# A transformer layer with expert retrieval: gathered rows of v from the end of u's loop on, and their sums emptied five chunks ahead of the end

## The chip, the cores and the metric

The kernel runs on one core of one Trainium2 chip. The metric is the device time of one execution in microseconds (us). TensorE (PE) multiplies matrices, VectorE (DVE) and ScalarE (ACT) do elementwise work, GpSimd (POOL) does some of that and issues the gathers, and SyncE (SP) issues most of the large loads.

## The reference

One layer over 256 tokens of width 1024: a mixer (retention beside block attention, merged by gates), and behind it the part that matters here, a product-key retrieval of experts (PEER). Each token picks 128 of 16384 experts (8 heads, 16 each); an expert is one row of u and one row of v:

```python
def one_chunk(args):
    hc, ec, gc = args                                  # tokens, chosen experts, gates
    u = u_tab[ec]
    a = jax.nn.gelu(jnp.einsum('td,thkd->thk', hc, u), approximate=False)
    return jnp.einsum('thk,thkd->td', gc * a, v_tab[ec])
```

The tables u and v are 16384 x 1024 float32 each.

## The kernel before

The tokens are shared between two ways of doing this.

**Dense.** For most tokens (NA = 128 columns in the product with u, ND = 176 in that with v) the kernel goes through the whole tables, in NK = 128 chunks of 128 experts. *u's loop* multiplies each chunk of u with the tokens (L1271) after its transposition on TensorE (L738, copied out by ACT in L739); ACT takes the gelu and POOL multiplies with the gates into W (L1228, L1229). Its last iterations also prepare v's first chunks. *v's loop* multiplies each chunk of v with W and adds up in PSUM. Since the product goes through two halves of reduced precision, each chunk of v is cut on ACT (the high half `rhi`, L148) and DVE (the low half `rlo`, L149), two chunks ahead of its use (`cut_v(c + 2)`), and W likewise once for two chunks (`cut_w`, L1243 and L1244). A chunk is eight pairs of matmuls (L1303, L1304). Six pairs of chunks (PLAIN) go uncut (L1301). The cut halves have four buffers each, the loaded chunks of both tables six (`raw_ring`). The two last chunks of v are done together, block by block, behind the loop, and each block goes through `add_up` (ACT L1349, DVE L1350) and `turn_back` (a transposition, DVE's adds, the writing of the result).

**Gathered.** For NG = 64 tokens all 128 rows of u and of v (as 64 gathers, two rows' worth of tokens in the 128 partitions), and for some more tokens extra gathers, are fetched by index from HBM: NU = 128 gathers of u, 128 rows of 4 KB each, and NV = 80 of v. A fetched tile of u is multiplied with the token and summed on DVE (`dot_v`, L1040). When all dots are done, their gelu and the gates give the weights `av` (L1100, L1101). A fetched tile of v is added to a running sum with its weight (L1115 on DVE; the first one of each sum is a copy on ACT, L1112). There are two running sums: `accx` (the first 16 tiles of v) and `vacc` (the other 64).

The fetched tiles lie in a ring of RING = 6. The gathers go by steps: `gather_step` does one fetch and one dot, or one fetch and one sum, as they come. A fetch is issued on POOL's queue and waits there until DVE is done with the tile that lay in its slot six fetches before; a sum waits on DVE until its tile has landed. Each engine works strictly in the order in which the program lists its instructions, so a step's place in the program sets what waits behind it. How many steps there are is set by a credit: `gather(n)` adds n and does a step for every whole unit. In u's loop n is 1.04 for each chunk, from the point where the top-16 of all tokens is done 1.2 (after a pause of four steps). In v's loop it is 0.65.

A dot of u begins when five tiles of u are outstanding, or when all of u are fetched; so the last four steps of u's part do a dot each and fetch nothing. The last six chunks of u's loop do no steps at all. In v's loop a step fetches until all 80 are fetched, and it sums when six tiles are outstanding or when all are fetched. In chunk NK - 8 = 120 all sums that are left are done at once. Behind them POOL loads the residual: `r0` (64 tokens, L1327), `r0b` (L1331), `r1` (128 tokens, L1332) and `upper`, the upper half of `vacc` (L1333). In chunk 123 `accx` is added to the PSUM sums by 16 matmuls (L1337). In chunk 124 DVE adds `vacc` to `r0` (L1340), in chunk 125 `upper` (L1342), and SP writes the 64 tokens out.

The code of the last chunks:

Of the kernel before, what the change touches and what calls it, by code (L numbers as in the profile page):

```python
# [28 lines left out]
NK = 128  # L29
# [8 lines left out]
RING = 6  # L38
# [25 lines left out]
NU = NJ + NX  # L64
# [12 lines left out]
def layer_kernel(ctx, tc, x, mix_norm_g, w_in, ret_w_branch, moba_q_gain, moba_k_gain, moba_w_branch,  # L77
# [640 lines left out]
    def load_to(i):  # L718
        while state["loaded"] < i + AHEAD + 2 * (i + AHEAD > sk_at):
            load_any(state["loaded"])  # L720
            state["loaded"] += 1

    def transpose_u(c):

        if c < NK and early_chunk(c):
            u_T[c] = u_raw.pop(c)
        elif c in TURN:
            r = u_raw.pop(c)
            u_T[c] = hi_tile(F32)
            for k in range(0, KC, 4):  # L730
                turn(u_T[c], r, slice(k, k + 4))
        elif c < NK:
            r = u_raw.pop(c)
            u_T[c] = hi_tile(F32)
            for q in range(2):
                p = side()
                for k in range(4):
                    T.transpose(p[:, k * P:(k + 1) * P], r.rearrange("p (i k) -> p k i", k=KC)[:, 4 * q + k], ident)  # L738
                A.activation(u_T[c][:, 512 * q:512 * (q + 1)], p, AF.Copy)  # L739
# [55 lines left out]
    for t in range(NT):  # L795
        for q in range(2):
            c = slice(512 * q, 512 * (q + 1))
# [109 lines left out]
    gs = {"n": 0, "u": 0, "dot": 0, "v": 0, "sum": 0, "rows": {}, "x": 0, "soft": False, "xdone": False, "later": [], "pause": 0, "pace": GATHER}  # L907
# [3 lines left out]
    v_order = [*range(NJ, NV), *range(NJ)]  # L911
# [104 lines left out]
    def chain_step(us):  # L1016

        credit["chain"] = min(credit["chain"], 0.0) + us
        while chain and credit["chain"] > 0:
            try:  # L1020
                credit["chain"] -= next(chain[0])
            except StopIteration:
                chain.pop(0)

    def fetch(tab, j):
        n = gs["n"] % RING
        gs["n"] += 1
        r = tk.tile([P, D], F32, name="rows_", bufs=2) if n >= 4 else hp_.tile([P, D], F32, name="rows", tag=("hl", "hh")[n % 2], bufs=2)
        G.indirect_dma_start(out=r, out_offset=None, in_=tab,  # L1029
                             in_offset=bass.IndirectOffsetOnAxis(ap=eg[:, j:j + 1], axis=0))  # L1030
        gs["rows"][j] = r
# [11 lines left out]
    def weights_x():  # L1043

        c = slice(NJ, NU)
        A.activation(av[:, c], av[:, c], AF.Gelu)
        gs["x"] = 0

        def product():
            V.tensor_tensor(av[:, c], av[:, c], gg[:, c], op=OP.mult)  # L1050
            nc.gpsimd.dma_start(gx[1].rearrange("n h i k -> (h i) n k"), av[:, c].rearrange("p (n k) -> p n k", n=NXG))
            after(2, back)

        def back():
            for n in range(NXV, NXG):
                nc.gpsimd.dma_start(x_rows(gates, n), gx[1][n].rearrange("h i k -> i h k"))
            gs["xdone"] = True

        after(2, product)
# [13 lines left out]
    def after(n, f):  # L1073
        gs["later"].append((n, f))

    def later():
        now, gs["later"] = gs["later"], []
        for n, f in now:
            f() if n <= 1 else after(n - 1, f)

    def gather_step():
        later()
        if gs["pause"] > 0:
            gs["pause"] -= 1
            return
        if gs["x"] == NX and gs["soft"]:
            weights_x()
        if gs["dot"] < NU:
            if gs["u"] < len(ready):
                fetch(peer_u[0], ready[gs["u"]])  # L1090
                gs["u"] += 1
            if gs["dot"] < gs["u"] and (gs["u"] - gs["dot"] == RING - 1 or gs["u"] == NU):
                j = ready[gs["dot"]]
                r = gs["rows"].pop(j)
                h = h2 if j < NJ else h2r[(j - NJ) // TOPK]
                after(1, partial(dot_v, j, r, h))
                gs["dot"] += 1
                if gs["dot"] == NU:
                    later()
                    A.activation(av[:, :NJ], av[:, :NJ], AF.Gelu)  # L1100
                    V.tensor_tensor(av[:, :NJ], av[:, :NJ], gg[:, :NJ], op=OP.mult)  # L1101
            return
        if gs["v"] < NV:
            fetch(peer_v[0], v_order[gs["v"]])
            gs["v"] += 1
        if gs["sum"] < gs["v"] and (gs["v"] - gs["sum"] == RING or gs["v"] == NV):
            j = v_order[gs["sum"]]
            r = gs["rows"].pop(j)
            if j in (0, NJ):
                a = cp.tile([P, D], F32, name="vacc", tag="h2") if j == 0 else tk.tile([P, D], F32, name="accx", tag="hx")  # L1110
                gs["acc" if j == 0 else "accx"] = a
                A.activation(a, r, AF.Copy, scale=av[:, j:j + 1])  # L1112
            else:
                a = gs["acc" if j < NJ else "accx"]
                V.scalar_tensor_tensor(a, r, av[:, j:j + 1], a, op0=OP.mult, op1=OP.add)  # L1115
            gs["sum"] += 1
# [46 lines left out]
    def gates_finish():  # L1163
        while full:
            gates_evac(*full.pop())
# [83 lines left out]
    def rows_x(n):  # L1249

        if n < NXG:
            h2r.append(lo_tile(F32))
            nc.scalar.dma_start(h2r[n], h2y[n].rearrange("h i d -> (h i) d"))

    for c in range(NK):
        load_to(len(pieces) + c + TAHEAD)
        rows_x(c)
        gates_finish()
        transpose_u(c + TAHEAD)
        if c and c % 2 == 0:  # L1260
            product_evac(c - 2, pa)
        if c == SCRATCH:
            while any(g in chain for g in topk_all):
                chain_step(1.0)
        if c % 2 == 0:
            pa = acc(0)
        uT = u_T.pop(c)
        hT = hTd if c in TURN or early_chunk(c) else hTf
        for k in range(KC):
            n = c % 2 * NA  # L1270
            T.matmul(pa[:, n:n + NA], uT[:, k * P:(k + 1) * P], hT[:, k], start=(c % 2 == 0 and k == 0),  # L1271
                     stop=(k == KC - 1), skip_group_check=True)
        pump()
        if c < NK - 6:
            gather(gs["pace"])
        chain_step(BUDGET)

        if c == NK - 4:
            while chain:
                chain_step(9.0)  # L1280
                gates_finish()
            cw = cp.tile([P, 2, D], F32R, name="cw", tag="b8")[:, :, :4 * ND].rearrange("p s (c t) -> p s c t", c=2)
        if c >= NK - 5:
            load_to(len(pieces) + c + 3)
        if c == NK - 3:
            cut_w(0)
            cut_v(0)
        elif c == NK - 2:
            cut_v(1)
# [17 lines left out]
    for c in range(NK):  # L1307
        load_to(len(pieces) + NK + c + 2)
        if (c + 2) // 2 not in PLAIN:
            cut_v(c + 2)  # L1310
            if c % 2 == 0:
                cut_w(c + 2)
        if c // 2 in PLAIN:
            cuts[c] = (v_raw.pop(c), None, W[:, c, :])
        else:
            cuts[c] = (*v_cut.pop(c), w_cut[c - c % 2][:, c % 2])
        if c < NK - 2:
            for b in range(KC):
                block(b, c)
            del cuts[c]  # L1320
        gather(GATHER_V)
        if c == NK - 8:
            while gs["sum"] < NV:
                gather_step()

            r0 = tk.tile([P, D], F32, name="rows_", bufs=2)
            nc.gpsimd.dma_start(r0[:NG], x1d[:NG, 0, :])  # L1327
            upper = hp_.tile([P, D], F32, name="rows", tag="hh", bufs=2)
            r1 = hp_.tile([P, D], F32, name="rows", tag="hh", bufs=2)
            r0b = oh_more.rearrange("p a b i j -> p (a b i j)").bitcast(F32)  # L1330
            nc.gpsimd.dma_start(r0b[:half], x1d[NG:, 0, :])  # L1331
            nc.gpsimd.dma_start(r1, x1d[:, 1, :])  # L1332
            nc.gpsimd.dma_start(upper[:NG], gs["acc"][NG:])  # L1333
        if c == NK - 5:

            for b in range(KC):
                T.matmul(o[b][:, 2 * ND:2 * ND + NXP], gs["accx"][:, b * P:(b + 1) * P], pick, start=False, stop=True,  # L1337
                         skip_group_check=True)
        if c == NK - 4:
            V.tensor_tensor(r0[:NG], r0[:NG], gs["acc"][:NG], op=OP.add)  # L1340
        if c == NK - 3:
            V.tensor_tensor(r0[:NG], r0[:NG], upper[:NG], op=OP.add)  # L1342
            nc.sync.dma_start(out_flat[:NG, :], r0[:NG])

# [81 lines left out]
```

## Time and profile before

| | |
|---|---|
| median of 3 runs | 962.13 us (961.7 to 962.34) |
| the profiled execution | 962.2 us |
| its span, first to last instruction | 960.4 us |
| TensorE busy | 942.4 us (98%) |
| VectorE busy | 794.3 us (83%) |
| ScalarE busy | 519.2 us (54%) |
| GpSimd busy | 393.9 us (41%) |
| HBM | 307.52 MB read, 334 GB/s over the span |
| mean granted clock of TensorE | 0.991 |

The times in the profile's rows count from the first instruction. u's loop ends and v's begins near 656 us. A row of a timeline is the start, the duration, the engine, the line, the operation, what is written from what, their sizes and the number of instructions in the row; in brackets stands how long the engine had been idle before it and what ended that. A row of the chain of waits is a start, a duration and what the time went to.

### The profile page before, as it was taken

To read this page: it belongs to the slowest core of one execution; us is meant where nothing else is said; L and a number is where in the kernel's file an instruction comes from. 1 tells how busy PE (TensorE), PEld (TensorE's weight loads), DVE (VectorE), ACT (ScalarE), POOL (GpSimd) and SP (SyncE) were. 2 spreads that over 40 slices of the span, in tenths; PEclk is the share of its full clock that TensorE was granted. 3 is DMA by queue.
4 is the path that set the end of the run, shared out by engine and by line. 5 is a ranking of instruction groups with operands and counts; after the bars stand their busy time and mean duration, and the time that the engine had idled before them with its cause. 6 is when DMAs were issued, how large, how long until landed. Compare 5 with 4: busy or idle time off the path is not lost.

```text
span 960.4 us, 19130 instructions
## 1 busy us (share of the span) xinstructions
PE 942.4 (98%) x7208; PEld 902.6 (94%) x7208; DVE 794.3 (83%) x1514; ACT 519.2 (54%) x956; POOL 393.9 (41%) x303
## 2 busy tenths in 40 slices
PE   8999999999999999999999999999999999999968
PEld 6887898998999999999999998999999999999967
DVE  6567567878679996999799999966798988989885
ACT  5554745544654345444577776966455454545431
POOL 3422010000204455344355675744375656566540
PEclk9999999999999999999999999999999999999987
DMA  9878879998898999999999999998999999999991
GB/s 318 234 191 246 231 223 279 308 308 247 250 396 330 408 360 341 397 359 393 367 369 378 405 367 360 344 361 277 377 409 386 408 378 409 386 393 397 379 332 45
DMA packets 109418, 320.40 MB, mean 334 GB/s; under 512 B 11372, under 2 KB 22517, under 8 KB 109198
## 3 DMA queue, kind: packets, MB, share of 16 engines
q1 hardware_dynamic: 64492, 184.43, 53.5%
q0 software_dynamic: 32512, 115.54, 32.3%
q10 hardware_dynamic: 12322, 19.21, 6.8%
q8 instruction: 57, 0.93, 0.4%
q14 instruction: 35, 0.29, 0.1%
HBM read 307.52 MB, written 13.14 MB: 334 GB/s over the span
## 4 chain that ended last, share of the span: by engine, by line
PE 57%; POOL 18%; issue 14%; DVE 6%; DMA 3%; ACT 1%; POOLq 0%; SPq 0%; DVEq 0%
PE acc L1271 17%; POOL rows L1029 11%; PE side L738 7%; PE acc L231 6%; PE acc L232 6%; PE acc L233 6%; PE acc L240 3%; PE acc L241 3%; PE acc L242 3%; DVE rows L1040 2%; DVE oh_more L1152 1%; DMA rows__5904<-in_peer_u_dram,eg 1%; DMA rows<-in_peer_v_dram,eg 1%; PE side L635 1%; DMA rows__6318<-in_peer_u_dram,eg 1%
## 5 line engine op out<-in xcount | busy, mean ns | idle before, releaser
L1029 POOL DMA_INDIRECT rows<-in_peer_v_dram,eg x54 | 106.9, 1980 | 73.9 <-DVE vacc L1115 48.3
L1029 POOL DMA_INDIRECT rows<-in_peer_u_dram,eg x86 | 103.7, 1205 | 80.6 <-DVE rows L1040 38.0
L738 PE MATMUL side<-ident,raw_ring 128*128 128x128 f32 x800 | 107.4, 277 | 0.4 <-ACT rhi__6591 L739 0.4
L738 PEld LDWEIGHTS side<-ident,raw_ring 128*128 128x128 f32 x800 | 96.9, 192 | 0.5 <-ACT rhi__6591 L739 0.5
L1243 ACT ACTIVATE cw<-W 128x352 fp32r<-128x352 f32 x58 | 28.9, 498 | 67.9 <-PE acc L1304 67.9
L1157 ACT ACTIVATE oh_buf<-oh_more,tS 128x128 bf16<-128x128 f16 x176 | 58.9, 428 | 0.2 <-DVE oh_more L1152 0.2
L1115 DVE SCALAR_TENSOR_TENSOR vacc<-rows,av,vacc 128x1024 f32<-128x1024 f32 x43 | 55.0, 1280 | 3.1 <-DMA rows<-in_peer_v_dram,eg 3.0
L1040 DVE SCALAR_TENSOR_TENSOR rows<-rows,h 128x1024 f32<-128x1024 f32 x43 | 52.7, 1236 | 3.3 <-DMA rows<-in_peer_u_dram,eg 3.3
L1229 POOL TENSOR_TENSOR W<-W,gl 128x256 f32<-128x256 f32 (+18 forms) x29 | 24.4, 842 | 55.6 <-ACT gl L1228 43.2
L1244 DVE TENSOR_TENSOR cw<-W,cw 128x352 fp32r<-128x352 f32 x58 | 30.2, 522 | 17.2 <-ACT cw L1243 16.4
L581 POOL DMA_DIRECT2D x1d<-xt x1 | 0.7, 657 | 88.5 <-DVE xt L563 88.5
L1214 ACT ACTIVATE W<-acc 128x512 f32<-128x512 f32 (+19 forms) x44 | 17.0, 387 | 34.6 <-DVE W L1212 28.9
L1152 DVE TENSOR_TENSOR oh_more<-iota,tI 128x1024 f16<-128x1024 f16 x44 | 33.8, 768 | 0.0
L1153 DVE TENSOR_TENSOR oh_buf<-oh_more,tM 128x1024 f16<-128x1024 f16 x44 | 31.7, 720 | 2.2
L155 POOL TENSOR_TENSOR gny<-va,minus_half 128x8 f32<-128x8 f32 x2 | 4.3, 2126 | 66.7 <-DVE va L455 66.7
L1271 PE MATMUL acc<-hTd,raw_ring 128*128 128x128 f32 x256 | 31.2, 275 | 0.0
L1271 PEld LDWEIGHTS acc<-hTd,raw_ring 128*128 128x128 f32 x256 | 29.9, 192 | 0.0
L1198 PE MATMUL acc<-oh_buf 128*128 128x128 bf16 x176 | 25.7, 219 | 1.5 <-ACT oh_buf L1157 0.7
L1199 PE MATMUL acc<-oh_buf 128*128 128x128 bf16 x176 | 25.7, 219 | 0.0
L1199 PEld LDWEIGHTS <-oh_buf 128*128 128x128 f16 x176 | 19.7, 114 | 3.3 <-issue 1.6
L1231 ACT ACTIVATE W<-acc 128x256 f32<-128x256 f32 (+18 forms) x53 | 19.2, 361 | 5.5 <-PE acc L1271 4.4
L1198 PEld LDWEIGHTS <-oh_buf 128*128 128x128 f16 x176 | 19.8, 114 | 0.0
(2701 smaller groups left out, 3494.0 us busy)
## 6 DMA issues: line engine op xcount, KB each, us to landing
raw_ring<-in_peer_v_dram SPq DMA_DIRECT2D x128, 512.0 KB
raw_ring<-in_peer_u_dram SPq DMA_DIRECT2D x100, 512.0 KB
raw_ring<-in_w_in_dram SPq DMA_DIRECT2D x52, 512.0 KB
raw_ring<-in_peer_w_q_dram SPq DMA_DIRECT2D x16, 512.0 KB
raw_ring<-turned SPq DMA_DIRECT2D x16, 512.0 KB
W<-in_peer_u_dram SPq DMA_DIRECT2D x12, 512.0 KB
eraw<-in_peer_u_dram ACTq DMA_DIRECT2D x32, 128.0 KB
h<-in_peer_u_dram ACTq DMA_DIRECT2D x32, 128.0 KB
```

Of the source, the lines that this page charges most:

```text
L231: T.matmul(o[t], xh[:, s], wh, start=(k == 0), stop=False)
L232: T.matmul(o[t], xh[:, s], wl, start=False, stop=False)
L233: T.matmul(o[t], xl[:, s], wh, start=False, stop=(k == kc - 1))
L738: T.transpose(p[:, k * P:(k + 1) * P], r.rearrange("p (i k) -> p k i", k=KC)[:, 4 * q + k], ident)
L1029: G.indirect_dma_start(out=r, out_offset=None, in_=tab, in_offset=bass.IndirectOffsetOnAxis(ap=eg[:, j:j + 1], axis=0))
L1040: V.scalar_tensor_tensor(r, r, 1.0, h, op0=OP.mult, op1=OP.mult, accum_out=av[:, j:j + 1])
L1115: V.scalar_tensor_tensor(a, r, av[:, j:j + 1], a, op0=OP.mult, op1=OP.add)
L1152: V.tensor_tensor(hot, iota4[:, None].to_broadcast(shape), tI[:, t, :, None, k:k + 4].to_broadcast(shape), op=OP.is_equal)
L1157: A.activation(o1[:, j], hot[:, 0, :, j], AF.Copy, scale=tS[:, t, k + j:k + j + 1])
L1198: T.matmul(p[:, j * P:(j + 1) * P], hi, o1, start=True, stop=False)
L1199: T.matmul(p[:, j * P:(j + 1) * P], lo, o1, start=False, stop=True)
L1271: T.matmul(pa[:, n:n + NA], uT[:, k * P:(k + 1) * P], hT[:, k], start=(c % 2 == 0 and k == 0), stop=(k == KC - 1), skip_group_check=True)
```

## The change

It has three parts. In a step at which all tiles of u are fetched but not all dots done, a tile of v is fetched, if the undone dots and the fetched tiles of v together leave a slot of the ring. In the last six chunks of u's loop the steps go on, if all dots are done and fewer than five tiles of v are outstanding. And the emptying of the sums moves from chunk 120 to chunk 123, with the loads of the residual behind it; the two adds to `r0` move from chunks 124 and 125 to 126 and 127. The 16 matmuls with `accx` stay in chunk 123.

```diff
@@ gather_step
             if gs["u"] < len(ready):
                 fetch(peer_u[0], ready[gs["u"]])
                 gs["u"] += 1
+            elif gs["u"] == NU and NU - gs["dot"] + gs["v"] < RING:
+                fetch(peer_v[0], v_order[gs["v"]])
+                gs["v"] += 1
             if gs["dot"] < gs["u"] and (gs["u"] - gs["dot"] == RING - 1 or gs["u"] == NU):
@@ u's loop
         pump()
-        if c < NK - 6:
+        if c < NK - 6 or gs["dot"] == NU and gs["v"] - gs["sum"] < RING - 1:
             gather(gs["pace"])
@@ v's loop
         gather(GATHER_V)
-        if c == NK - 8:
+        if c == NK - 5:
             while gs["sum"] < NV:
                 gather_step()
...
             nc.gpsimd.dma_start(upper[:NG], gs["acc"][NG:])
-        if c == NK - 5:
-
             for b in range(KC):
                 T.matmul(o[b][:, 2 * ND:2 * ND + NXP], gs["accx"][:, b * P:(b + 1) * P], pick, start=False, stop=True,
                          skip_group_check=True)
-        if c == NK - 4:
+        if c == NK - 2:
             V.tensor_tensor(r0[:NG], r0[:NG], gs["acc"][:NG], op=OP.add)
-        if c == NK - 3:
+        if c == NK - 1:
             V.tensor_tensor(r0[:NG], r0[:NG], upper[:NG], op=OP.add)
             nc.sync.dma_start(out_flat[:NG, :], r0[:NG])
```

## The prediction

> **What bounds the kernel now.** I read the page's shares first, then a table of stretches, then the timelines of TensorE (PE), VectorE (DVE), GpSimd (POOL) and ScalarE (ACT) at the two places that the change touches.
>
> ```profile
> span 960.4 us, 19130 instructions
> PE 942.4 (98%) x7208; PEld 902.6 (94%) x7208; DVE 794.3 (83%) x1514; ACT 519.2 (54%) x956; POOL 393.9 (41%) x303
> ```
> ```profile
> 640.00:657.00 17.00, 17.00 (x153) 17.00 (x153) 6.44 (x10) 9.06 (x20) 2.96 (x3) 1.00 0.71 228
> 700.00:720.00 20.00, 20.00 (x149) 20.00 (x148) 19.82 (x21) 11.51 (x14) 14.77 (x6) 1.00 1.03 409
> 929.80:935.20 5.40, 0.04 (x1) 0.04 (x1) 3.58 (x4) 0.00 (x0) 0.52 (x1) 0.50 0.77 149
> 935.20:946.90 11.70, 11.70 (x49) 11.70 (x50) 7.67 (x8) 1.44 (x2) 0.00 (x0) 0.50 0.21 46
> ```
>
> The columns are the stretch, its length, the busy time of PE, weight load, DVE, ACT and POOL, the granted clock, the DMA share and GB/s. TensorE is full nearly everywhere. In v's loop, DVE (19.82 of 20) and DMA (1.03) are full beside it. At the end of u's loop DMA has room (0.71). The one large hole in PE is 929.8 to 935.2, followed by 11.7 us at half clock. Both lie where the gathered sums are emptied:
>
> ```profile
> 922.59 0.36 PE L1303 MATMUL side<-cw,rhi__10164 128*128 128x352 f32 x1
> 924.77 0.35 PE L1303 MATMUL side<-cw,rhi__10188 128*128 128x352 f32 x1
> 926.95 0.36 PE L1303 MATMUL side<-cw,rhi__10229 128*128 128x352 f32 x1
> 935.16 0.52 PE L1304 MATMUL side<-cw,rlo__10230 128*128 128x176 f32 x1 [7.86 <-DVE rlo__10230 L149]
> 939.02 1.79 PE L1337 MATMUL side<-pick,accx 128*128 128x16 f32 x8
> 942.36 0.64 PE L1303 MATMUL side<-cw,rhi__10250 128*128 128x352 f32 x1
> 946.49 0.55 PE L1303 MATMUL side<-cw,rhi__10272 128*128 128x352 f32 x1
> 948.87 0.35 PE L1303 MATMUL side<-cw,rhi__10300 128*128 128x352 f32 x1
> ```
> ```profile
> 920.36 1.22 DVE L149 TENSOR_TENSOR rlo__10189<-raw_ring,rhi__10188 128x1024 fp32r<-128x1024 f32 x1
> 921.93 1.28 DVE L1115 SCALAR_TENSOR_TENSOR vacc<-rows,av,vacc 128x1024 f32<-128x1024 f32 x1
> ...
> 932.69 1.28 DVE L1115 SCALAR_TENSOR_TENSOR vacc<-rows,av,vacc 128x1024 f32<-128x1024 f32 x1 [1.82 <-DMA rows<-in_peer_v_dram,eg]
> 933.89 1.22 DVE L149 TENSOR_TENSOR rlo__10230<-raw_ring,rhi__10229 128x1024 fp32r<-128x1024 f32 x1
> 940.28 1.21 DVE L1340 TENSOR_TENSOR rows__10221<-rows__10221,vacc 64x1024 f32<-64x1024 f32 x1
> 942.55 1.21 DVE L1342 TENSOR_TENSOR rows__10221<-rows__10221,rows 64x1024 f32<-64x1024 f32 x1
> ```
>
> Seven sums stand in a row on DVE from 921.93 (first and last shown), the last of them waiting for a gathered row. Chunk 123's low half (rlo__10230) stands behind them, so PE, which began that chunk at 926.95, stops for 7.86 us. The clock then falls, and chunk 124 takes 942.36 to 946.49, 4.13 us, where chunk 121 took 922.59 to 924.77, 2.18 us. The two last chunks, which are done together, begin at 948.87.
>
> **The change, part by part.** *How far the rows get ahead.* In u's loop the pace 1.04 is paid for 62 chunks (the code switches in chunk 61) and 1.2 for 60: 64.48 + 72.0 = 136.48, so 136 steps by chunk 121 (128 fetches, 4 pauses, 4 steps that drain the dots) and a credit of 0.48. Each of the 4 draining steps now fetches a row of v too (undone dots plus v rows are 4, under the ring's 6). Chunk 122 adds 1.2, one step: the fifth row. Then 5 rows are outstanding and the new condition (under 5) stops it. V's loop starts with 5 rows fetched, none summed, credit 0.68. Before, after s steps s rows were fetched and s − 5 summed; now s + 5 are fetched and s summed. Before, chunk 120 had 0.48 + 0.65 × 121 = 79.1, so 79 steps and 74 sums, its own and six emptied: the seven seen. Now the 80th sum needs 0.68 + 0.65 × (c + 1) ≥ 80, chunk 122, and the last fetch (step 75) is in chunk 114. The emptying, moved to chunk 123, finds nothing left. That holds for any credit, as 0.65 × 124 = 80.6.
>
> *What goes.* Sums 75 to 80 spread over chunks 115 to 122 at the old pace, so chunk 123's low half follows in its turn. From 926.95, at full clock: chunk 123, 2.18; the 16 matmuls of L1337, 942.36 − 939.02 = 3.34 at half clock, so 1.67; chunks 124 and 125, 4.36. Together 8.21, so the last two begin at 935.16 and not at 948.87: 13.7 us saved. The 11.5 us behind them stay.
>
> *The rule on the clock.* The Trainium skill, page "TensorE: Matmul & The Clock Gate", Part 1, says that the clock is gated after about 3.4 us of idleness and comes back after about 3.4 us of sustained work. The trace has 11.7 us of full work at 0.50 behind the stop, more than three times that; by the page the slow part would have cost 3.4 / 2 = 1.7 us, and the gain would be 7.9 + 1.7 = 9.6 us. The measured stretch decides the sum.
>
> *What the five fetches cost in u's loop.* On POOL, ahead of what is queued there:
>
> ```profile
> 633.22 1.25 POOL L1029 DMA_INDIRECT rows<-in_peer_u_dram,eg  x1 [0.16 <-issue]
> 638.28 0.73 POOL L1229 TENSOR_TENSOR W<-W,gl 128x256 f32<-128x256 f32 x1 [3.81 <-ACT gl L1228]
> 646.88 0.74 POOL L1229 TENSOR_TENSOR W<-W,gl 128x256 f32<-128x256 f32 x1 [7.88 <-ACT gl L1228]
> ```
> ```profile
> 645.31 0.26 ACT L1100 ACTIVATE av<-av 128x64 f32<-128x64 f32 x1 [4.14 <-DVE rows L1040]
> 645.47 1.07 ACT L739 ACTIVATE rhi__7333<-side 128x512 f32<-128x512 f32 x2
> 648.28 1.95 PE L1271 MATMUL acc<-hTf,rhi__7333 128*128 128x128 f32 x16
> ```
>
> A fetch there is 1.25 us. The fetches of rows 0 and 1 stand between the last u row (633.22) and the product at 638.28, rows 2 and 3 ahead of that at 646.88, where POOL idles 3.81 and 7.88 us: covered. A fetch first waits until the dot of the row six before is done (its ring slot); those are dots of rows 122 to 126, one or more steps old. Without that cover each would delay the products, and through them the release of PSUM, by at most its 1.25 us. The five rows are 2.6 MB, 6.4 us at 409 GB/s, in 17 us with a DMA share of 0.71, so 4.9 us of room in it. The loads on SP's queue get slower by that, but each is issued six chunks of 2.7 us ahead. The place to watch is ACT at 645.31: it stands 4.14 us for the last dot, which waits for its row; the next transposed chunk is out at 646.54 and needed at 648.28, 1.74 us of room. The new rows stand behind that row in POOL's queue, so I take 0; the other bound is a landing 6.4 us later, a stop of 4.7 us.
>
> *What five earlier sums cost at the start of v's loop.* The first is a copy on ACT in chunk 0, the others are DVE's from chunk 2 on, where DVE had no sums before:
>
> ```profile
> 659.54 1.21 DVE L149 TENSOR_TENSOR rlo__7499<-raw_ring,rhi__7498 128x1024 fp32r<-128x1024 f32 x1
> 663.03 0.24 PE L1304 MATMUL side<-cw,rlo__7499 128*128 128x176 f32 x1
> 674.34 1.13 ACT L1112 ACTIVATE accx<-rows,av 128x1024 f32<-128x1024 f32 x1
> 846.47 0.52 DVE L1244 TENSOR_TENSOR cw<-W,cw 128x352 fp32r<-128x352 f32 x1
> 846.90 1.28 DVE L1115 SCALAR_TENSOR_TENSOR vacc<-rows__9278,av,vacc 128x1024 f32<-128x1024 f32 x1
> 848.10 1.22 DVE L149 TENSOR_TENSOR rlo__9453<-raw_ring,rhi__9452 128x1024 fp32r<-128x1024 f32 x1
> 849.24 1.22 DVE L149 TENSOR_TENSOR rlo__9474<-raw_ring,rhi__9473 128x1024 fp32r<-128x1024 f32 x1
> ```
>
> Chunk 3's low half is ready at 660.75 and used at 663.03: 2.28 us of room. The copy (1.13) comes ahead of its cut on ACT and leaves 1.15. From then on DVE's work for two chunks, by the distances of starts in the last four rows, is 2 × 1.14 for the cuts, 0.43 for the weights' half and 1.3 sums × 1.20: 4.27 us, against 4.36 on PE. So the room does not shrink, and I take 0; if it fails, four sums by chunk 6 at 1.28, less 1.15, stop PE for up to 4.0 us.
>
> *The end.* The residual's loads are now issued for chunk 123, and the two adds to r0 stand on DVE in chunks 126 and 127, right ahead of the first add_up.
>
> ```profile
> 928.91 0.57 POOL L1332 DMA_DIRECT2D rows<-x1d  x1 [2.44 <-DMA rows<-in_peer_v_dram,eg]
> 934.27 0.52 POOL L1333 DMA_DIRECT2D rows<-vacc  x1 [4.79 <-DVE vacc L1115]
> 923.48 9.12 DMA rows<-in_peer_v_dram,eg
> ```
> ```profile
> 949.61 0.33 ACT L1349 ACTIVATE turned<-side 128x192 f32<-128x192 f32 x1 [8.85 <-PE side L1304]
> ```
>
> Two chunks take 4.36 us, so chunk 124's low half follows that at 920.36 at 924.7, and the last sum runs from about 926.3 to 927.6. The load of r1 waited for a ring slot and that of upper for vacc; both now wait for this last sum and are issued by 928.7 (0.57 and 0.52). DVE comes to upper's add about 933.4, and the first add_up is due about 936.1 (935.16, one block of 0.54, ACT's copy of 0.33). If upper takes as long as the slowest row shown, 9.12 us from the chain of waits, it is there at 937.8 and its add (1.21) ends at 939.0: 2.9 us late. That row was measured with gathers and other loads around it in POOL's queue; here the gathers ended in chunk 114. So 0 is taken, 2.9 is the other bound.
>
> *The sum.* 960.4 − 13.7 = 946.7 us of span; with the 1.8 us around it (962.2 in all) 948.5, and as the median of the runs, 962.13, is the same within 0.1 us, 948.4. With half a microsecond for the small covers together: 948.8.
>
> **The rivals.** *The room at the start of v's loop or at the end fails.* For it speaks that DVE is full (19.82 of 20); against it that the old steady state runs at the same load without a stop. Price 0.5 to 4.0 us: 949 to 952.5.
>
> *The half clock is not, or not wholly, the stop's doing* but belongs to the end, and stays. Against it: it begins 2.5 us after the last matmul (927.31), within the stop. If it stays, only the stop of 7.86 goes: 954.3. By the page named above, 3.4 us of the slow work are the stop's and the rest has another cause: 952.5.
>
> *The emptying only moves.* If the rows land later than the pace assumes, sums are left at chunk 123, and the same stop comes there, three chunks from the end. Each leftover sum costs 1.28 us, and from a stop of 2.5 us on the clock falls: 2 to 3 leftovers give back 2.6 to 3.9 us and up to 5.9 us of half clock, 955 to 958. Against it: the ring keeps five rows ahead, 7.7 chunks or 17 us, and the slowest landing shown is 9.12.
>
> *Slower: the last dot comes late at the turn.* If five more rows share the DMA, ACT stands longer at 645.31, the transposed chunk is late, PE stops and the clock falls (11.7 us at half lose 5.9). To eat the 13.7 us the stop must be 7.8 us, the landing 9.5 us late; the whole of the five rows is 6.4 us of transfer. At 10.5 us late: 963.5.
>
> *The change doesn't do what it says*: a fetch needs u counted to its end and a ring slot, and both are there for four steps by the count. If none were fetched early, seven sums would stand at chunk 123 as before at 120: no change, 962.
>
> **How the numbers follow.** The forecast holds 0.70 (its own range 946 to 950), failing room 0.15, the clock 0.04, the moved emptying 0.05, slower 0.03, no effect 0.03. The range 945.5 to 953.0 holds the first two; the others, 0.15, are left out. A difference of 0.2%, 1.9 us, is about what a measurement tells from none: faster 0.94, same 0.03, slower 0.03.
>
> **What would show it.** Right: no idle time of PE over 2 us after 656; clock 1.00 to the end of the last blocks; five gathers of v on POOL between 634 and 650 and the last near 900; single sums on DVE, each between cuts, to the end; chunk 123 at its old time. Wrong: a stop of PE between 640 and 665; several L1115 in a row near the end; add_up waiting on upper or r0 on DVE; ACT waiting longer than 4.14 us at L1100; half clock without a stop.

## The result: 1.4% faster, as the tail's stop and its half clock are gone

The changed kernel takes 948.33 us (median of 4 runs, 947.73 to 948.95), the kernel before 961.91 us (961.52 to 962.34). The ratio is 0.9859, with a 95% interval from 0.9842 to 0.9876. Forecast were 948.8 us. One later run of the kernel before took 1522.59 us at a granted clock of 0.556; it counts in no ratio and no group of runs here.

The page of the changed kernel (its lines behind 1091 stand three further down, so L1115 is now L1118, L1303 and L1304 are L1306 and L1307; from the 16 matmuls on it is one, so L1337 is now L1338):

```profile
span 947.2 us, 19130 instructions
PE 937.3 (99%) x7208; PEld 897.5 (95%) x7208; DVE 791.8 (84%) x1514; ACT 519.2 (55%) x956; POOL 386.8 (41%) x303
```

The span is 13.2 us shorter. Span less busy time of TensorE was 960.4 − 942.4 = 18.0 us and is 9.9: 8.1 us less idle, the stop. Busy time fell from 942.4 to 937.3 with the same 7208 matmul instructions: 5.1 us, near the 5.9 that 11.7 us of work at half clock lose. The stretches at the turn and at the end:

```profile
640.00:657.00 17.00, 17.00 (x155) 17.00 (x154) 6.80 (x10) 9.06 (x19) 6.39 (x6) 1.00 0.99 388
915.00:926.90 11.90, 11.90 (x89) 11.90 (x89) 11.05 (x11) 7.49 (x10) 0.56 (x1) 1.00 1.02 351
926.90:935.20 8.30, 8.30 (x66) 8.30 (x65) 8.21 (x9) 2.52 (x4) 0.52 (x1) 1.00 0.21 59
```

TensorE is full where it stood (8.30 of 8.30), at clock 1.00. At the end of u's loop the DMA share went from 0.71 to 0.99 at no cost to TensorE. In the timelines of TensorE and VectorE near the end, chunk 123 (rlo__10222) and what surrounds it:

```profile
927.33 0.36 PE L1306 MATMUL side<-cw,rhi__10221 128*128 128x352 f32 x1
929.51 0.99 PE L1338 MATMUL side<-pick,accx 128*128 128x16 f32 x8
931.25 0.40 PE L1306 MATMUL side<-cw,rhi__10242 128*128 128x352 f32 x1
935.66 0.35 PE L1306 MATMUL side<-cw,rhi__10300 128*128 128x352 f32 x1
```
```profile
923.75 1.28 DVE L1118 SCALAR_TENSOR_TENSOR vacc<-rows,av,vacc 128x1024 f32<-128x1024 f32 x1
924.94 1.22 DVE L149 TENSOR_TENSOR rlo__10222<-raw_ring,rhi__10221 128x1024 fp32r<-128x1024 f32 x1
926.08 1.23 DVE L149 TENSOR_TENSOR rlo__10243<-raw_ring,rhi__10242 128x1024 fp32r<-128x1024 f32 x1
927.21 0.53 DVE L1247 TENSOR_TENSOR cw<-W,cw 128x352 fp32r<-128x352 f32 x1
927.65 1.29 DVE L1118 SCALAR_TENSOR_TENSOR vacc<-rows,av,vacc 128x1024 f32<-128x1024 f32 x1
...
932.68 1.22 DVE L1341 TENSOR_TENSOR rows__10285<-rows__10285,vacc 64x1024 f32<-64x1024 f32 x1
933.93 1.22 DVE L1343 TENSOR_TENSOR rows__10285<-rows__10285,rows 64x1024 f32<-64x1024 f32 x1
936.76 0.34 DVE L1351 TENSOR_TENSOR turned<-turned,side 128x176 f32<-128x176 f32 x1 [1.61 <-ACT turned L1350]
```

Single sums stand between the cuts. The last (927.65) belongs to chunk 122; nothing is left for the emptying. The last two chunks begin at 935.66 instead of 948.87: 13.2 us, the whole difference of the spans.

### The profile page after: what moved, and what is told of

Read it like the earlier page. It is cut to its first block, busy times and chain, and to the rows that moved or that the text cites. A ratio compares the mean times of both kernels' runs of the same rounds, so it can differ in the third digit from the quotient of the medians.

```text
span 947.2 us, 19130 instructions
## 1 busy us (share of the span) xinstructions
PE 937.3 (99%) x7208; PEld 897.5 (95%) x7208; DVE 791.8 (84%) x1514; ACT 519.2 (55%) x956; POOL 386.8 (41%) x303
## 4 chain that ended last, share of the span: by engine, by line
PE 85%; DVE 4%; POOL 4%; issue 4%; DMA 3%; ACT 0%; SPq 0%; DVEq 0%; POOLq 0%
PE acc L1274 17%; PE acc L1306 9%; PE side L1306 9%; PE side L738 8%; PE acc L231 6%; PE acc L232 6%; PE acc L233 6%; PE acc L1307 4%; PE side L1307 4%; PE acc L240 3%; PE acc L241 3%; PE acc L242 3%; DMA rows<-in_peer_u_dram,eg 2%; PE side L1304 2%; PE acc L1304 2%
## 5 line engine op out<-in xcount | busy, mean ns | idle before, releaser
L1029 POOL DMA_INDIRECT rows<-in_peer_v_dram,eg x54 | 98.6, 1826 | 71.8 <-DVE vacc L1118 54.1
L1118 DVE SCALAR_TENSOR_TENSOR vacc<-rows,av,vacc 128x1024 f32<-128x1024 f32 x43 | 55.1, 1281 | 0.1
```

Source lines behind the costliest of these rows:

```text
L1029: G.indirect_dma_start(out=r, out_offset=None, in_=tab, in_offset=bass.IndirectOffsetOnAxis(ap=eg[:, j:j + 1], axis=0))
```

## The experiments

**Which part carries the gain.** The early fetches alone, with the end as in the kernel before (against the changed kernel):

```diff
-        if c == NK - 5:
+        if c == NK - 8:
             while gs["sum"] < NV:
                 gather_step()
...
+        if c == NK - 5:
             for b in range(KC):
...
-        if c == NK - 2:
+        if c == NK - 4:
             V.tensor_tensor(r0[:NG], r0[:NG], gs["acc"][:NG], op=OP.add)
-        if c == NK - 1:
+        if c == NK - 3:
```

> The early fetches alone; the emptying stays in chunk 120, the adds to r0 in 124 and 125. My theory: with 5 rows ahead chunk 120 has done 79 steps and 79 sums, one is left and its row was fetched in chunk 114, so there is no stop and all of the gain stays: 948.4 us (947.5 to 949.5). Rival, that the later emptying carries the gain: a stop of several us stays in front of chunk 123, 954 or more.

Measured: 949.28 us (948.34 to 951.61), ratio 0.9887 (0.9856 to 0.9918). The waits of TensorE hold no stop near the end. Run once more for a closer number:

> The early fetches alone once more, for a closer number: 949.28 us so far, where the changed kernel has 948.33 and 948.04. My theory, that the moved emptying adds nothing: within 1.9 us of 948.2. Rival, that the two adds to r0 or a residual load earlier in the loop cost something: 949.5 or more.

Measured: 948.09 us (947.7 to 949.16, 6 runs), ratio 0.9885 (0.9858 to 0.9912). In this run's timelines of VectorE and TensorE, the two sums of chunk 120 (its own and the one left) and chunk 123's cut (rlo__10230):

```profile
922.73 2.60 DVE L1118 SCALAR_TENSOR_TENSOR vacc<-rows,av,vacc 128x1024 f32<-128x1024 f32 x2
925.25 1.22 DVE L149 TENSOR_TENSOR rlo__10230<-raw_ring,rhi__10229 128x1024 fp32r<-128x1024 f32 x1
```
```profile
926.58 0.29 PE L1307 MATMUL side<-cw,rlo__10230 128*128 128x176 f32 x1
```

The cut is ready at 926.47, 0.11 us before its use, and TensorE does not wait. In the changed kernel the same cut is ready 1.37 us before its use (926.16, used at 927.53). So moving the emptying buys room for chunk 123 (the time from a cut being ready to its use), which was not needed here. The changed kernel itself, once more:

> The changed kernel once more, as the measure for the other runs beside it: 948.3 us, 13.6 less than before.

Measured: 948.04 us (946.98 to 949.18), ratio 0.987 (0.9843 to 0.9897). So the early fetches alone carry the gain; moving the emptying adds nothing that shows in the time. The other way round, only the end moved:

> The emptying and what stands behind it in chunk 123, and the adds in 126 and 127, without the early fetches. My theory: chunk 123 has done 81 steps and 76 sums, four are left, the last row is fetched some 3 us before and lands 6 to 9 us later; the cuts of chunks 126 and 127 and the residual's add wait behind it. PE stops 2 to 5 us ahead of the last two chunks and the end runs partly at half clock: 952 to 958. Rival, that the place of the emptying is what counts: 948.4.

Measured: 953.82 us (952.41 to 954.13), ratio 0.9926 (0.9898 to 0.9954). That is also faster than before, but 5.5 us short of the changed kernel's 948.33. VectorE's timeline, then TensorE's waits in that run:

```profile
928.18 1.27 DVE L1115 SCALAR_TENSOR_TENSOR vacc<-rows__10113,av,vacc 128x1024 f32<-128x1024 f32 x1
929.49 5.25 DVE L1115 SCALAR_TENSOR_TENSOR vacc<-rows,av,vacc 128x1024 f32<-128x1024 f32 x4
934.65 1.22 DVE L149 TENSOR_TENSOR rlo__10301<-raw_ring,rhi__10300 128x1024 fp32r<-128x1024 f32 x1
```
```profile
PE side L1353 <- DVE turned L1348: 1.7, 1, 1.7
PE side L1303 <- DVE cw L1244: 1.1, 1, 1.1
```

Five sums in a row, chunk 123's own and the four that the count leaves, stand ahead of chunk 126's cut. The stop is shorter than in the kernel before, since only two chunks still have to be cut and the rest has run ahead, but the clock still falls. The wait of 1.1 us stands ahead of chunk 126; the one of 1.7 us stands behind the first two blocks of the last two chunks, as VectorE does the two adds to `r0` (937.36 to 939.83) ahead of add_up. In the table of stretches:

```profile
934.80:938.20 3.40, 1.90 (x12) 1.42 (x11) 3.40 (x4) 0.32 (x1) 0.52 (x1) 1.00 0.53 148
938.20:945.00 6.80, 5.09 (x23) 4.73 (x22) 4.10 (x13) 1.34 (x5) 0.00 (x0) 0.50 0.19 41
```

**Whether the half clock is the stop's doing.** In the kernel before, matmuls that nobody reads fill the stop, into free columns of a PSUM bank:

```diff
+        if c == NK - 5:
+            for i in range(69):
+                T.matmul(o[0][:, 384:512], ident, ident, start=False, stop=False, skip_group_check=True)
         if c < NK - 2:
             for b in range(KC):
                 block(b, c)
```

> The kernel before with 69 extra matmuls of 128x128 (into columns of a bank that nobody reads) ahead of chunk 123, about 8.2 us of work, which fill the stop. My theory, that the half clock is the stop's doing: the clock stays at 1.00, chunks 123 to 125 and the 16 matmuls go at full speed and 5.5 to 5.9 of the 13.7 us go without the stop's cause being touched: 956 to 956.8. Rival, that the half clock belongs to the end of the kernel: no change, 962.

Measured: 963.73 us, ratio 1.0029 (1.0009 to 1.0049): a miss by the size of the filling. The clock stayed at 1.00, but the 69 matmuls took nearly twice what I had put:

```profile
927.83 15.60 PE L1319 MATMUL side<-ident 128*128 128x128 f32 x138
943.78 0.36 PE L1303 MATMUL side<-cw,rhi__10229 128*128 128x352 f32 x1
```

Each stands in the trace as two instructions (as do the eight of L1337, the "16 matmuls" so far), and chunk 123 begins at 943.78, 8 us after its cut. With half of them:

> The kernel before with 34 extra matmuls in the stop instead of 69. The 69 took 15.6 us, 0.23 each, and chunk 123 began 8 us later than its cut was ready; but the clock stayed at 1.00. 34 take 7.7 us and end about when the cut is ready: the last two chunks begin 8.1 us after 935.2, 943.3 instead of 948.9. My theory, that the stop costs the half clock: 956 to 957. Rival: 962.

Measured: 956.38 us (955.07 to 959.68, 12 runs), ratio 0.9959 (0.9938 to 0.9979). In its timeline of TensorE and its table of stretches:

```profile
925.82 7.78 PE L1319 MATMUL side<-ident 128*128 128x128 f32 x68
933.36 0.41 PE L1303 MATMUL side<-cw,rhi__10229 128*128 128x352 f32 x1
937.73 0.41 PE L1303 MATMUL side<-cw,rhi__10250 128*128 128x352 f32 x1
939.96 0.36 PE L1303 MATMUL side<-cw,rhi__10272 128*128 128x352 f32 x1
```
```profile
927.00:945.00 18.00, 17.62 (x143) 17.17 (x142) 13.40 (x17) 2.44 (x5) 1.09 (x2) 1.00 0.46 100
```

The burst of sums is untouched and the result still waits for it, yet 4.5 us are gone (the kernel before was at 960.91 beside it); a little less than forecast. Chunk 124 takes 2.23 us (937.73 to 939.96) where it took 4.13. The mean granted clock is 0.998 or more in all 12 runs, where it was 0.989 to 0.996 in the 17 of the kernel before. So the half clock belongs to the stop, not to the end of the kernel. Eight of those 17 runs had a clock of 0.994 or more, that is, a shorter slow stretch; against the nine others (median 962.15) the filling gains 5.8 us, as forecast.

**What a stop costs.** The changed kernel with N extra operations of a sum's length (two, four or six) on VectorE ahead of chunk 123's cut:

```diff
+        if c == NK - 7:
+            hold_ = hTf.rearrange("p k t -> p (k t)")
+            for i in range(N):
+                V.scalar_tensor_tensor(hold_, hold_, 1.0, hold_, op0=OP.mult, op1=OP.max)
         if (c + 2) // 2 not in PLAIN:
             cut_v(c + 2)
```

> The changed kernel with two extra operations on VectorE ahead of chunk 123's cut: 2.5 us less 1.37 of room, a stop of 1.1 us. My theory: too short for the clock to fall, so its price is its length: 949.2. If any stop brings the half clock: 950.8 or more.

> The same with four operations, 5.0 us less 1.37, a stop of 3.6 us. My theory: the clock falls as in the stop of 7.9 us, and the slow stretch, which so far lasted 6.8, 13.7 and 17.1 us, costs half of the work in it: 948.2 + 3.6 + 2 to 6, so 954 to 958. If the clock holds through a stop of this length: 951.8.

> The changed kernel with six extra operations of a sum's length on VectorE ahead of chunk 123's cut, 7.2 us, of which 1.37 us are room that chunk 123 has there: PE stops for 5.8 us. My theory: the clock falls about 2.5 us into the stop and stays at half for about 17 us, over 11 us of work: 5.8 + 5.6 us more than 948.4, 959 to 961. Rival, by the Trainium skill's page on the clock gate (3.4 us of work bring the clock back): 5.8 + 1.7, about 956. If the half clock is not the stop's doing: 954.2.

Measured: 948.78 us (948.5 to 949.9) with two, 955.89 (951.12 to 958.42) with four, 959.64 (956.23 to 961.77) with six; ratios 0.9892 (0.9865 to 0.992), 0.9966 (0.9944 to 0.9988) and 0.9986 (0.9967 to 1.0005). The stop in TensorE's timeline, in that order:

```profile
926.96 0.35 PE L1307 MATMUL side<-cw,rlo__10224 128*128 128x176 f32 x1 [0.66 <-DVE rlo__10224 L149]
```
```profile
930.04 0.35 PE L1307 MATMUL side<-cw,rlo__10226 128*128 128x176 f32 x1 [3.64 <-DVE rlo__10226 L149]
```
```profile
932.24 0.51 PE L1307 MATMUL side<-cw,rlo__10228 128*128 128x176 f32 x1 [5.48 <-DVE rlo__10228 L149]
```

Against 948.2, between the two medians of the changed kernel, a stop of 0.66 us costs about its length, 0.6 us, which is within the spread. One of 3.64 costs 7.7 us in the median and one of 5.48 costs 11.4: stop and half clock again. No run of the changed kernel stood beside these; the early fetches alone, on the chip of the first two, took 948.09. With four operations the time follows, by and large, the clock that each run was granted: the run of 951.12 us had 1.000 and cost only its stop (2.9 us), 953.17 (the one in the profile) and 953.7 had 0.998, and the five from 957.34 on had 0.992 to 0.995. The slow stretch with six operations (its idle part and its working part), and then with four:

```profile
930.40:932.20 1.80, 0.00 (x0) 0.00 (x0) 1.80 (x3) 0.00 (x0) 0.00 (x0) 0.50 0.00 0
932.20:944.00 11.80, 11.76 (x49) 11.76 (x50) 9.03 (x9) 1.45 (x2) 0.52 (x1) 0.50 0.20 44
```
```profile
930.60:934.00 3.40, 3.40 (x17) 3.40 (x16) 3.40 (x5) 0.26 (x1) 0.52 (x1) 0.50 0.00 0
```

**What bounds it now.** With TensorE full, PLAIN pairs, which go uncut to spare VectorE, cost TensorE 4.77 us instead of 4.36:

```diff
-PLAIN = [6 + 10 * i for i in range(6)]
+PLAIN = []        # the other: [6 + 20 * i for i in range(3)]
```

> The changed kernel with all chunks of v cut (PLAIN empty). TensorE bounds it now: an uncut pair takes 4.77 us, a cut one 4.36, so 6 x 0.41 = 2.5 us go if VectorE (4.27 us of work for 4.36) and the loads (397 GB/s asked) keep up: 946. Rival, that the uncut pairs are the relief that the gathers need: cuts come late again and again, 948 to 953.

> The changed kernel with three uncut pairs instead of six. If VectorE keeps up: 1.2 us less, 947.1. If the relief is needed: room runs out between the pairs that are left, 948 to 951.

Measured: 945.55 us (944.97 to 946.44), ratio 0.9841 (0.9815 to 0.9868), and 946.71 (946.26 to 947.41), ratio 0.9854 (0.9827 to 0.9881), beside 948.04 for the changed kernel on the same chip: 2.5 and 1.3 us less. VectorE is full, or nearly, in the stretches of the first, and TensorE still does not stop:

```profile
660.00:700.00 40.00, 40.00 (x295) 40.00 (x295) 40.00 (x41) 23.64 (x30) 29.10 (x12) 1.00 1.01 392
760.00:900.00 140.00, 140.00 (x1029) 140.00 (x1029) 137.92 (x139) 80.64 (x97) 99.94 (x43) 1.00 1.01 399
```

The same with one chunk more kept for the end:

```diff
-        if c < NK - 2:
+        if c < NK - 3:
...
-        for c in (NK - 2, NK - 1):
+        for c in (NK - 3, NK - 2, NK - 1):
```

> The changed kernel without uncut pairs (945.55 us) and with the last three chunks done block by block at the end instead of the last two, so that TensorE has more work under each block's way back. A block's matmuls are then 0.81 us beside 0.75 us of VectorE's, instead of 0.54: 0.5 to 0.8 us less, 944.9, which is less than a measurement tells. If the way back is not covered by it: 945.5.

Measured: 944.5 us (943.94 to 945.7), ratio 0.9849 (0.9822 to 0.9876) to the kernel before, which was at 958.36 beside it. That is the lowest time here; its distance of 1.0 us from 945.55 is of the forecast sign, but the two did not run side by side and it is too small to be called shown.

## Why the prediction was right, step by step

**The count.** It held. Five gathers of v stand on POOL in u's loop, at 635.22, 637.11, 639.74, 641.83 and 648.07, where POOL was idle in the kernel before. The first and the last of them, the last fetch of v, and the loads of `r0`, `r1` and `upper`:

```profile
635.22 1.59 POOL L1029 DMA_INDIRECT rows<-in_peer_v_dram,eg  x1 [0.30 <-DVE oh_buf L1156]
...
648.07 0.97 POOL L1029 DMA_INDIRECT rows<-in_peer_v_dram,eg  x1
...
905.72 1.68 POOL L1029 DMA_INDIRECT rows<-in_peer_v_dram,eg  x1 [2.85 <-DVE vacc L1118]
909.65 0.56 POOL L1330 DMA_DIRECT2D rows__10285<-x1d  x1 [2.25 <-DVE vacc L1118]
...
921.42 0.56 POOL L1335 DMA_DIRECT2D rows<-x1d  x1 [10.67 <-DVE vacc L1118]
929.23 0.52 POOL L1336 DMA_DIRECT2D rows<-vacc  x1 [7.25 <-DVE vacc L1118]
```

**The sum.** From chunk 123's start to the last two chunks it had 8.21 us; measured are 935.66 − 927.33 = 8.33. The 16 matmuls had 1.67, and took 929.51 to 931.25, 1.74. Chunk 123 starts 0.38 us later than before (927.33 against 926.95), which was there before the first early fetch: the last fetch of u is at 633.67, 0.45 later than in the other trace.

**The turn.** ACT waited 4.07 us for the last dot, not 4.14, although DMA is full there now. The bound of 4.7 us was not needed: the last u row came no later for v's rows queued behind it.

```profile
645.61 0.26 ACT L1103 ACTIVATE av<-av 128x64 f32<-128x64 f32 x1 [4.07 <-DVE rows L1040]
```

**The start of v's loop.** The copy on ACT left chunk 3 1.49 us of room (cut at 661.92, used at 663.41; 1.15 was forecast), and no chunk of it stopped. Cutting everything at once later showed that the steady state holds even without the uncut pairs.

**The end: one point was wrong.** I had the residual's loads issued for chunk 123 and r1's waiting for the last sum. POOL has nothing else left in its queue and runs ahead: r0's load went at 909.65, when the ring slot was free, r1's at 921.42. Only upper's, at 929.23, waited for the last sum, which ran from 927.65 (926.3 was forecast), and its add at 933.93 waited for nothing. That cost no time here, but the early loads share DMA with v's. The smallest room in the changed loop is at chunk 121, where ACT's cut waited for its load (rows of ACT, VectorE and TensorE):

```profile
919.67 1.06 ACT L148 ACTIVATE rhi__10176<-raw_ring 128x1024 fp32r<-128x1024 f32 x1 [1.05 <-DMA raw_ring<-in_peer_v_dram]
```
```profile
921.04 1.22 DVE L149 TENSOR_TENSOR rlo__10177<-raw_ring,rhi__10176 128x1024 fp32r<-128x1024 f32 x1
```
```profile
923.17 0.24 PE L1307 MATMUL side<-cw,rlo__10177 128*128 128x176 f32 x1
```

Its low half is ready at 922.26 and used at 923.17: 0.91 us. r1's load, at 921.42, went out after that cut had begun; whether r0's, ten us before, takes some of the room was not tried.

**The clock: right in kind, partly luck in size.** The half clock was the stop's doing, as the filled stop shows, and so it went with the stop. Its price was taken from one profile, and that was of a run with a long slow stretch (mean granted clock 0.991). Beside the experiments the kernel before ran 52 times on three chips: 25 runs had 0.991 or less and took 960.83 to 966.65 us (median 962.28), 19 had 0.996 and took 956.13 to 960.16 (median 957.36), and 8 lay between. The four runs beside the result were all near 962. From a profile of the other kind the same sum would have given a gain some 5 us smaller, by these medians. So that the 13.7 us of the sum met the result's 13.6 is owed in part to those four runs, whose times are of the long kind like the profile's; on the chip where the kernel before had a median of 958.36 the early fetches alone gained some 10 us.

## What to carry to other kernels

When one engine is 98% busy, look at where its other 2% lie in time; here 8 of the 18 us were one hole, and the half clock behind it cost 5 to 6 more in that profile. A burst of catching up at the end of a loop is cured where its lag begins: five fetches in a stretch with DMA to spare took it away, while moving the burst kept part of it. And once the hole is gone, relief that was built in for another engine is worth testing again: dropping the uncut pairs gave 2.5 us more. (Whether they were needed before the hole was gone was not tried.)

## What the hardware showed that I had not expected

The slow stretches differ in length: 17.1 us in the kernel before, 13.7 with six operations, 6.8 with the moved emptying, 3.4 with four operations, near enough to 5, 4, 2 and 1 times 3.41 us. The Trainium skill's page "TensorE: Matmul & The Clock Gate", Part 1, has a free-running window of 3.4 us and lets one busy window bring the clock back. The run with four operations agrees with that, and there the clock fell at 930.6, after the stop had ended at 930.04. The other three took more windows, the longest with TensorE full for 11.7 us of them.

Nor did the clock need one long stop to fall. With the moved emptying, TensorE was busy for 1.90 of the 3.40 us before the fall. The profile with six operations has a second slow stretch, in u's loop, behind 3.41 us in which TensorE was idle for 1.58 us, 1.47 of them at once:

```profile
578.83:582.24 3.41, 1.83 (x17) 1.39 (x16) 3.36 (x7) 2.66 (x9) 0.45 (x1) 1.00 1.02 408
582.24:585.65 3.41, 3.41 (x19) 3.41 (x18) 3.17 (x9) 2.02 (x9) 2.57 (x3) 0.50 0.66 243
```

So a stop's price varies from run to run, and the runs with four operations spread over 7.3 us (951.12 to 958.42) where those of the changed kernel spread over 2.2. What decides the number of windows stays open.
